# Multi-query attention: small copies ahead of the later loads, a different order of the query buffers, and GpSimd in program order

## The chip, the cores and the metric

The kernel runs on one core of a Trainium2 chip. The metric is the device time of one execution in microseconds, start to end. Before the change three runs took 775.3, 776.2 and 777.91 us, so the median is 776.2 us. The profile comes from one execution more, which took 776.08 us; its span from the first to the last instruction is 774.3 us.

Engines are named as in the profile: PE is the matrix engine (PEld its weight loads), ACT the scalar engine, DVE the vector engine, POOL GpSimd, SP the sync engine, which here only issues DMAs. A "q" behind an engine's name is its sequencer, which issues DMAs and waits on semaphores.

## The reference

There are 8 batches with 16 heads of 64 elements and 1024 positions. Keys and values have one head, shared by all query heads.

```python
# q: (8, 1024, 16, 64) float32; k, v: (8, 1024, 64) float32
q = q.transpose(0, 2, 1, 3)                       # (8, 16, 1024, 64)
scores = np.matmul(q, k[:, None].transpose(0, 1, 3, 2)) / np.sqrt(64)
weights = np.exp(scores - np.max(scores, axis=-1, keepdims=True))
weights = weights / np.sum(weights, axis=-1, keepdims=True)
out = np.matmul(weights, v[:, None]).transpose(0, 2, 1, 3)
```

## The kernel before

**Tiling.** Heads are taken two at a time, which makes 8 pairs in a batch and 64 pairs (p = 0 to 63) in all. For each pair the keys are cut into 8 tiles of 128. One score tile holds 128 keys on the partitions against 512 query positions of both heads; so a pair has 16 score tiles (8 key tiles, 2 query halves). `score` (L391) makes one with two matmuls, one per head, from `k2t` (the transposed keys, twice one above the other, one copy for each head of the pair) and `qt` (the transposed queries). The exponential of a score tile is made either on ACT (`exp_act`, L404) or on DVE by bit operations and two products (`exp_dve`, L409). The weights are then multiplied with the values in `value` (L438), where a column of ones gives the sums, and `reciprocal` and `normalise` (L458, L463) divide and store a pair's output with one DMA from SP.

**What sets the order.** `plan` (L51) is a planner in plain Python, with costs for each operation; it returns a list of operations, and the loop at L516 issues them one by one. Under `tc.manual_schedule` the instructions of PE, ACT and DVE stay in exactly this program order. POOL and SP are not in that set before the change: a scheduler orders their instructions by itself, as early as it sees fit, and can put one ahead of another that the program names first.

**Staging of queries.** Queries go through two pools of two buffers each: `qn` (natural layout, fp16) and `qt` (transposed). `load_q` (L337) issues a DMA from POOL's queue that also casts to fp16. `trans_q` (L347) issues a transposing DMA from SP's queue. Pairs 0 and 1 are each loaded alone; from pair 2 on one load and one transpose carry two pairs (`quad`, L328), so load 2 is that of pairs 2 and 3. `begin` (L491), called before the first score of a pair w, issues for even w the load of w + 4 and the transpose of w + 2. It also issues a batch ahead: the two DMAs of the next keys on POOL at the third pair of a batch (`load_k`, L299), the values on SP at the fifth (`load_v`, L308), the transpose of the keys on SP and the scaling of the values on DVE at the sixth (`trans_k`, L321, `scale_v`, L313).

**The start.** `load_first` (L356) brings batch 0's keys (`kn`) and pair 0's queries (`qf`) as fp32, plainly, without a DMA that casts or transposes. `kn` comes on SP's queue, the two halves of `qf` on ACT's and SP's. POOL casts the keys into one half of `k16` (L367). `turn_first` (L372) casts them into the other half on DVE, casts `qf` to `qn[0]` half by half on DVE, transposes on PE, and copies out of PSUM on ACT (keys) and DVE (queries). Then the first score can run.

**Who gets which buffer.** A tile gets one of its pool's buffers when its first access comes in the order of the schedule, not where its name is made. Before the change the loads of pairs 1 and 2 (L511, L512) and the transpose of pair 1 (L513) come ahead of `turn_first` (L515) in the program. Load 1 and load 2 so take the two `qn` buffers, and `qn[0]`, first written by the cast at L386, comes into the buffer of load 1 when the transpose of pair 1 has read it. In the built program, the cast of the first half of `qf` waits for three things: its own load, load 1, and the transpose of pair 1.

**Other buffers.** The output tiles (`osb`) have three buffers, and `kn` and `qf` take two of these at the start. `vn`, the raw values, has one.

Of the kernel before, what the change touches and what calls it, by code (L numbers as in the profile page):

```python
# [9 lines left out]
FP32 = mybir.dt.float32  # L10
# [4 lines left out]
ENG = mybir.EngineType  # L15

P = 128
# [229 lines left out]
def kernel(  # L247
# [7 lines left out]
    nc = tc.nc  # L255
    B, S, H, D = q.shape
    assert D == 64 and S == 1024 and H % 4 == 0
    NKT = S // P
# [9 lines left out]
    kvp = ctx.enter_context(tc.tile_pool(name="kvp", bufs=2))  # L268
    qp = ctx.enter_context(tc.tile_pool(name="qp", bufs=2))
# [37 lines left out]

    def load_v(b):  # L308
        st = kst[b]
        st["vn"] = kvp.tile([P, NKT, D], FP32, tag="vn", bufs=1, name=f"vn{b}")  # L310
        nc.sync.dma_start(out=st["vn"], in_=v[b].rearrange("(p c) d -> p c d", p=P))

    def scale_v(b):  # L313
# [14 lines left out]
    def quad(p):  # L328

        return (p,) if p < 2 else (p & ~1, p | 1)  # L330

    def queries(pool, tag, p, more):

        t = pool.tile([P, 2 * NKT + more, P], FP16, tag=tag, name=f"{tag}{p}")
        return t[:, 0 : NKT * len(quad(p)), :]

    def load_q(p):  # L337
        ps = quad(p)
        b, hp = divmod(ps[0], HP)
        qn[ps[0]] = queries(qp, "qn", p, 0)  # L340
        nc.gpsimd.dma_start(  # L341
            out=qn[ps[0]].rearrange("p (c r) x -> p c (r x)", r=len(ps)),
            in_=q[b, :, 2 * hp : 2 * hp + 2 * len(ps), :].rearrange(
                "(c p) h d -> p c (h d)", p=P),
        )

    def trans_q(p):  # L347
        ps = quad(p)
        t = queries(qtp, "qt", p, 1)
        nc.sync.dma_start_transpose(  # L350
            out=t, in_=qn[ps[0]].rearrange("p c x -> p (c x)")
        )
        for r, x in enumerate(ps):
            qt[x] = t.rearrange("p (c r) x -> p c r x", r=len(ps))[:, :, r, :]

    def load_first():  # L356
        st = kst.setdefault(0, {})
        kn = osbp.tile([P, NKT, D], FP32, tag="osb", name="kn")
        nc.sync.dma_start(out=kn, in_=k[0].rearrange("(p c) d -> p c d", p=P))
        st["qf"] = osbp.tile([P, NKT, 2 * D], FP32, tag="osb", name="qf")  # L360
        for c in range(NQC):
            (nc.scalar, nc.sync)[c].dma_start(
                out=st["qf"][:, 4 * c : 4 * c + 4, :],
                in_=q[0, QC * c : QC * c + QC, 0:2, :].rearrange("(c p) h d -> p c (h d)", p=P),
            )
        st["k16"] = kvp.tile([P, NKT, 2, D], FP16, tag="k16", name="k160")
        nc.gpsimd.tensor_copy(out=st["k16"][:, :, 1, :], in_=kn)  # L367
        st["kn"] = kn
        qn[0] = queries(qp, "qn", 0, 0)
        qt[0] = queries(qtp, "qt", 0, 1)  # L370

    def turn_first():  # L372

        st = kst[0]
        k16 = st["k16"]
        kps = psp.tile([P, NKT, P], FP16, tag="acc0", name="kps")
        qps = psp.tile([P, NKT, P], FP16, tag="acc1", name="qps")
        st["k2t"] = kvp.tile([P, NKT + 1, P], FP16, tag="k2t", name="k2t0")[:, 0:NKT, :]
        nc.vector.tensor_copy(out=k16[:, :, 0, :], in_=st["kn"])  # L379
        for c in range(NQC):  # L380
            x = slice(4 * c, 4 * c + 4)
            for i in range(4 * c, 4 * c + 4):
                nc.tensor.transpose(  # L383
                    kps[:, i, :], k16[:, i, :, :].rearrange("p r d -> p (r d)"), ident)
            nc.scalar.copy(out=st["k2t"][:, x, :], in_=kps[:, x, :])  # L385
            nc.vector.tensor_copy(out=qn[0][:, x, :], in_=st["qf"][:, x, :])  # L386
            for i in range(4 * c, 4 * c + 4):
                nc.tensor.transpose(qps[:, i, :], qn[0][:, i, :], ident)  # L388
            nc.vector.tensor_copy(out=qt[0][:, x, :], in_=qps[:, x, :])

    def score(t, c, s):  # L391
        p, j = divmod(t, NKT)
        sc[t, c] = psp.tile([P, 2, QC], FP32, tag=f"sc{s}", name=f"sc{t}_{c}")
        for h in range(2):
            nc.tensor.matmul(  # L395
                sc[t, c][:, h, :],
                kst[p // HP]["k2t"][64 * h : 64 * h + 64, j, :],
                qt[p][64 * h : 64 * h + 64, 4 * c : 4 * c + 4, :],
                start=True, stop=True, tile_position=(64 * h, 0),
            )  # L400
        if t not in wt:
            wt[t] = wtp.tile([P, 2, S], FP16, tag="wt", name=f"wt{t}")

    def exp_act(t, c):  # L404
        nc.scalar.activation(
            out=wt[t][:, :, c * QC : (c + 1) * QC], in_=sc.pop((t, c)), func=EXP, scale=ascale
        )

    def exp_dve(t, c):  # L409

        name = f"{t}"
        if c == 0:
            zs[t] = dvp.tile([P, 2, S], U16, tag="z", bufs=ZBUFS, name=f"z{name}")
        z = zs[t]
        nc.vector.tensor_scalar(
            out=z[:, :, c * QC : (c + 1) * QC], in0=sc.pop((t, c)), scalar1=vscale,
            scalar2=(15 + math.log2(C0)) * ONE, op0=ALU.mult, op1=ALU.add,
        )  # L420
        if c == 0:
            return
        V = nc.vector
        u = dvp.tile([P, 2, S], U16, tag="u", name=f"u{name}")
        m = ms[t] = dvp.tile([P, 2, S], FP16, tag="m", bufs=ZBUFS, name=f"m{name}")
        h = u.bitcast(FP16)
        steps[t] = (
            lambda: V.tensor_scalar(
                out=wt[t].bitcast(U16), in0=z, scalar1=0xFC00, scalar2=None,
                op0=ALU.bitwise_and),  # L430
            lambda: V.tensor_scalar(
                out=u, in0=z, scalar1=1023, scalar2=14 << 10,
                op0=ALU.bitwise_and, op1=ALU.bitwise_or),
            lambda: V.tensor_tensor(out=m, in0=h, in1=h, op=ALU.mult),
            lambda: V.tensor_tensor(out=m, in0=z.bitcast(FP16), in1=m, op=ALU.mult),
        )

    def value(p, grp, j, k, n, end, s):  # L438


        if n == 0:
            acc[p, grp] = psp.tile([P, QC], FP32, tag=f"acc{s}", name=f"acc{p}_{grp}")
        t = NKT * p + j
        w = (wt[t], zs[t].bitcast(FP16), ms[t])[k] if t in zs else wt[t]
        for x in range(BLOCKS[grp], BLOCKS[grp + 1]):
            i, h = divmod(x, 2)
            o = (x - BLOCKS[grp]) * (D + 1)
            nc.tensor.matmul(  # L448
                acc[p, grp][:, o : o + D + 1], w[:, h, i * P : (i + 1) * P],
                kst[p // HP]["v"][k][:, j, 0 : D + 1],  # L450
                start=(n == 0 and o == 0), stop=end, skip_group_check=True,
            )
# [5 lines left out]
    def reciprocal(p, grp):  # L458
        a = blocks(p, grp)
        rec[p, grp] = recp.tile([P, 8], FP32, tag="rec", name=f"rec{p}_{grp}")  # L460
        nc.vector.reciprocal(out=rec[p, grp][:, 0 : a.shape[1]], in_=a[:, :, D])  # L461
# [29 lines left out]
    def begin(w):  # L491
        if w % 2 == 0:
            if w + 4 < NP:
                load_q(w + 4)
            if w + 2 < NP:
                trans_q(w + 2)
        if w == 1:
            scale_v(0)
        b, hp = divmod(w, HP)
        if b + 1 < B:  # L500
            if hp == 2:
                load_k(b + 1)
            if hp == 4:
                load_v(b + 1)
            if hp == HP - 3:
                trans_k(b + 1)
                scale_v(b + 1)

    load_first()
    load_v(0)  # L510
    load_q(1)  # L511
    load_q(2)  # L512
    trans_q(1)  # L513
    with tc.manual_schedule(engines={ENG.PE, ENG.Activation, ENG.DVE}):
        turn_first()  # L515
        for _, _, (op, *args) in plan(NP, NKT)[0]:  # L516
            if op == "qk":
                while begun <= args[0] // NKT:
                    begin(begun)
                    begun += 1  # L520
                score(*args)
            elif op == "act":
                exp_act(*args)
            elif op == "z":
                exp_dve(*args)
            elif op == "step":
                steps[args[0]][args[1]]()
            elif op == "av":
                value(*args)
            elif op == "rec":  # L530
                reciprocal(*args[:2])
            else:
                normalise(*args[:2])
# [27 lines left out]
```

The softmax here doesn't subtract the row's maximum and nothing guards it: scores larger than these inputs give would overflow.

## Time and profile before

| what | measured |
|---|---|
| time, median of three runs | 776.2 us (775.3 to 777.91) |
| span of the profiled execution | 774.3 us |
| busy: ACT, PE, DVE, POOL | 750.3, 738.5, 720.4, 45.1 us |
| first exponential on ACT starts | 18.31 us |
| mean granted clock of PE | 0.991 |
| bytes moved by DMA | 75.06 MB, mean 97 GB/s |

How to read it: a busy share is a mean over the whole span, while each stage has its own limit. A row of the timeline gives the start, the duration, the engine, the line and the operation, then output and inputs by the program's names; in square brackets it gives the idle time of the engine before it and what ended that wait. The chain of work that ended last follows the releases backwards from the last instruction. The granted clock of PE is given as a share of the full one. Matmul ends are modelled, so a busy PE need not be one at its peak.

DMA landings, from issue to landing, in the first 60 us: `kn` 3.4 us, the halves of `qf` 4.2 and 4.6 us, `vn` 4.9 us, load 1 6.5 us, load 2 7.0 us, the transpose of pair 1 7.1 us.

### The profile page before, as it was taken

How to read it: one execution, taken by the hardware profiler on the slowest of the kernel's cores; microseconds unless marked ns; L12 is line 12 of the kernel's file. 1: busy time of each engine (PE TensorE's matmuls, PEld its weight loads, DVE VectorE, ACT ScalarE, POOL GpSimd, SP SyncE). 2: the span in 40 equal slices, each digit the busy share in tenths (PEclk: the TensorE clock that was granted, in tenths of full speed). 3: DMA queues.
4: the chain of work that ended last, by engine and by line, in shares of the span. 5: the costliest groups of instructions: out<-in, count | busy, mean ns of one | idle time of the engine just before them, and what ended most of it. 6: DMA issues, size and time to landing. Idle time of an engine off the chain costs nothing.

```text
span 774.3 us, 29944 instructions
## 1 busy us (share of the span) xinstructions
PE 738.5 (95%) x13616; PEld 486.3 (63%) x13616; DVE 720.4 (93%) x1043; ACT 750.3 (97%) x817; POOL 45.1 (6%) x59
## 2 busy tenths in 40 slices
PE   1899999999999999999999999999999999999997
PEld 1266666666666666666666666666666666666676
DVE  1999999999999999999999999999999999999982
ACT  1999999999999999999999999999999999999996
POOL 3100001000100001000010000000000000000000
PEclk9699999999999999999999999999999999999999
DMA  9944456556465557645585354646454546441312
GB/s 137 121 83 90 94 95 97 112 97 111 101 94 90 111 91 124 102 80 100 109 111 111 83 98 84 124 83 111 97 89 94 103 90 111 86 82 57 84 57 84
DMA packets 189839, 75.06 MB, mean 97 GB/s; under 512 B 90256, under 2 KB 188560, under 8 KB 189712
## 3 DMA queue, kind: packets, MB, share of 16 engines
q1 hardware_dynamic: 141072, 54.40, 31.4%
q0 software_dynamic: 47840, 18.35, 21.7%
q8 instruction: 106, 1.74, 1.0%
q10 hardware_dynamic: 800, 0.39, 0.2%
q14 instruction: 21, 0.17, 0.1%
HBM read 39.58 MB, written 33.55 MB: 94 GB/s over the span
## 4 chain that ended last, share of the span: by engine, by line
ACT 50%; PE 27%; DVE 16%; issue 6%; DMA 2%; POOL 0%; DVEq 0%; POOLq 0%; ACTq 0%
DMA qt_114<-qn_110 1%; DMA qn_110<-in_q_dram 1%; PE acc_0_262 L448 0%; PE acc_2_1390 L448 0%; PE acc_0_15309 L448 0%; PE acc_0_7689 L448 0%; PE acc_0_14463 L448 0%; PE acc_0_16447 L448 0%; PE acc_0_12219 L448 0%; PE acc_0_2902 L448 0%; PE acc_0_9676 L448 0%; PE acc_0_884 L448 0%; PE acc_2_16627 L448 0%; PE acc_0_17281 L448 0%; PE acc_2_17178 L448 0%
## 5 line engine op out<-in xcount | busy, mean ns | idle before, releaser
L395 PEld LDWEIGHTS <-k2t_120 64*128 64x128 f16 x256 | 13.0, 96 | 23.0 <-issue 18.4
L395 PEld LDWEIGHTS <-k2t_14746 64*128 64x128 f16 x256 | 12.8, 93 | 11.9 <-issue 6.2
L395 PEld LDWEIGHTS <-k2t_12480 64*128 64x128 f16 x256 | 12.6, 93 | 11.1 <-issue 5.3
L395 PEld LDWEIGHTS <-k2t_5706 64*128 64x128 f16 x256 | 12.6, 93 | 11.0 <-issue 5.2
L395 PEld LDWEIGHTS <-k2t_1194 64*128 64x128 f16 x256 | 12.4, 93 | 11.0 <-issue 5.4
L395 PEld LDWEIGHTS <-k2t_10207 64*128 64x128 f16 x256 | 12.4, 93 | 10.9 <-issue 5.3
L395 PEld LDWEIGHTS <-k2t_3433 64*128 64x128 f16 x256 | 12.4, 93 | 10.8 <-issue 5.2
L395 PEld LDWEIGHTS <-k2t_7972 64*128 64x128 f16 x256 | 12.2, 93 | 10.3 <-issue 4.9
L385 ACT COPY k2t_120<-kps 128x512 f16<-128x512 f16 x2 | 1.2, 586 | 13.6 <-PE kps L383 13.6
L388 PE MATMUL qps<-ident,qn_106 128*128 128x128 f16 x8 | 1.2, 308 | 10.4 <-DVE qn_106 L386 10.4
L386 DVE CAST qn_106<-qf 128x512 f16<-128x512 f32 x2 | 0.8, 421 | 10.6 <-DMA qt_114<-qn_110 10.6
L388 PEld LDWEIGHTS <-qn_106 128*128 128x128 f16 x8 | 0.7, 131 | 10.9 <-DVE qn_106 L386 10.9
L383 PE MATMUL kps<-ident,k_104 128*128 128x128 f16 x8 | 1.2, 311 | 5.1 <-POOL k_104 L367 5.1
L379 DVE CAST k_104<-kn 128x512 f16<-128x512 f32 x1 | 0.4, 427 | 4.1 <-DMA kn<-in_k_dram 4.1
L383 PEld LDWEIGHTS <-k_104 128*128 128x128 f16 x8 | 0.8, 142 | 5.1 <-POOL k_104 L367 5.1
L461 DVE RECIPROCAL rec_2_17786<-acc_2_17697 128x6 f32<-128x6 f32 x1 | 0.2, 196 | 2.6 <-PE acc_2_17697 L448 2.6
L341 POOL DMA_DIRECT2D qn_7122<-in_q_dram x1 | 1.3, 1292 | 22.7 <-DMA qt_6554<-qn_5975 22.7
L341 POOL DMA_DIRECT2D qn_1487<-in_q_dram x1 | 1.2, 1236 | 23.0 <-DMA qt_956<-qn_410 23.0
L341 POOL DMA_DIRECT2D qn_10514<-in_q_dram x1 | 1.2, 1237 | 22.9 <-DMA qt_9939<-qn_9357 22.9
L341 POOL DMA_DIRECT2D qn_8818<-in_q_dram x1 | 1.2, 1207 | 23.0 <-DMA qt_8250<-qn_7664 23.0
L461 DVE RECIPROCAL rec_0_17874<-acc_0_17769 128x6 f32<-128x6 f32 x1 | 0.2, 195 | 2.5 <-PE acc_0_17769 L448 2.5
L341 POOL DMA_DIRECT2D qn_5429<-in_q_dram x1 | 1.3, 1320 | 20.8 <-DMA qt_4858<-qn_4279 20.8
(5811 smaller groups left out, 3449.5 us busy)
## 6 DMA issues: line engine op xcount, KB each, us to landing
qn_112<-in_q_dram POOLq DMA_DIRECT2D x1, 512.0 KB, 7.0
qn_144<-in_q_dram POOLq DMA_DIRECT2D x1, 512.0 KB, 7.4
qn_410<-in_q_dram POOLq DMA_DIRECT2D x1, 512.0 KB, 6.4
qn_954<-in_q_dram POOLq DMA_DIRECT2D x1, 512.0 KB, 5.6
out_dram<-osb_450 SPq DMA_DIRECT2D x1, 512.0 KB, 4.4
out_dram<-osb_746 SPq DMA_DIRECT2D x1, 512.0 KB, 4.4
qn_1487<-in_q_dram POOLq DMA_DIRECT2D x1, 512.0 KB, 7.5
out_dram<-osb_1075 SPq DMA_DIRECT2D x1, 512.0 KB, 3.2
```

Source lines behind the costliest of these rows:

```text
L341: nc.gpsimd.dma_start(out=qn[ps[0]].rearrange("p (c r) x -> p c (r x)", r=len(ps)), in_=q[b, :, 2 * hp : 2 * hp + 2 * len(ps), :].rearrang ...
L379: nc.vector.tensor_copy(out=k16[:, :, 0, :], in_=st["kn"])
L383: nc.tensor.transpose(kps[:, i, :], k16[:, i, :, :].rearrange("p r d -> p (r d)"), ident)
L385: nc.scalar.copy(out=st["k2t"][:, x, :], in_=kps[:, x, :])
L386: nc.vector.tensor_copy(out=qn[0][:, x, :], in_=st["qf"][:, x, :])
L388: nc.tensor.transpose(qps[:, i, :], qn[0][:, i, :], ident)
L395: nc.tensor.matmul(sc[t, c][:, h, :], kst[p // HP]["k2t"][64 * h : 64 * h + 64, j, :], qt[p][64 * h : 64 * h + 64, 4 * c : 4 * c + 4, :], ...
L461: nc.vector.reciprocal(out=rec[p, grp][:, 0 : a.shape[1]], in_=a[:, :, D])
```

## The change

It has four parts.

- `load_first` now makes the tiles of pair 1's queries (`qn[1]`) and of the values (`vn`) itself, and two copies of 128x1 elements on POOL write one column of each: the first from `kn`, the second from `qf`. The loads that later fill these tiles write the same place, and so have to wait for the copies, which in turn wait for `kn` and for the first half of `qf`. `load_q` and `load_v` make their tiles only if there is none yet.
- Both halves of `qf` are now issued from ACT's queue.
- Load 2 and the transpose of pair 1 come behind `turn_first` in the program. By the first access, pair 1's tile now takes one `qn` buffer and pair 0's the other, and load 2 gets pair 0's when the casts are transposed. In the built program the cast of the first half of `qf` waits for the load of that half only. SP's order is then `kn`, values, transpose of pair 1, and so on.
- POOL joins the engines that keep program order. In the built order POOL's loads of the keys of batches 1 to 7 now each stand behind the query loads that the program names first. Before, the keys of batch 1 stood directly behind load 2, those of batches 2 and 3 around load 4, and each later one well over a batch ahead of its use; now they are issued within the batch ahead. SP is still ordered by the scheduler, and the transposes of the keys stand there nearly as before: for batch 2 between the stores of pairs 5 and 6, for batch 1 now between the transposes of loads 2 and 4 instead of ahead of both.

The orders of PE, ACT and DVE do not change, but for the second issue of `qf` on ACT.

```diff
     def load_v(b):
         st = kst[b]
-        st["vn"] = kvp.tile([P, NKT, D], FP32, tag="vn", bufs=1, name=f"vn{b}")
+        if "vn" not in st:
+            st["vn"] = kvp.tile([P, NKT, D], FP32, tag="vn", bufs=1, name=f"vn{b}")
         nc.sync.dma_start(out=st["vn"], in_=v[b].rearrange("(p c) d -> p c d", p=P))
...
     def load_q(p):
         ps = quad(p)
         b, hp = divmod(ps[0], HP)
-        qn[ps[0]] = queries(qp, "qn", p, 0)
+        if p not in qn:
+            qn[p] = queries(qp, "qn", p, 0)
         nc.gpsimd.dma_start(
...
         for c in range(NQC):
-            (nc.scalar, nc.sync)[c].dma_start(
+            nc.scalar.dma_start(
                 out=st["qf"][:, 4 * c : 4 * c + 4, :],
...
         st["kn"] = kn
         qn[0] = queries(qp, "qn", 0, 0)
+        qn[1] = queries(qp, "qn", 1, 0)
+        st["vn"] = kvp.tile([P, NKT, D], FP32, tag="vn", bufs=1, name="vn0")
+        for x, y in ((qn[1][:, 0, 0:1], kn), (st["vn"][:, 0, 0:1], st["qf"])):
+            nc.gpsimd.tensor_copy(out=x, in_=y[:, 0, 0:1])
         qt[0] = queries(qtp, "qt", 0, 1)
...
     load_first()
     load_v(0)
     load_q(1)
-    load_q(2)
-    trans_q(1)
-    with tc.manual_schedule(engines={ENG.PE, ENG.Activation, ENG.DVE}):
+    with tc.manual_schedule(engines={ENG.PE, ENG.Activation, ENG.DVE, ENG.Pool}):
         turn_first()
+        load_q(2)
+        trans_q(1)
         for _, _, (op, *args) in plan(NP, NKT)[0]:
```

## The prediction

> **What bounds the kernel now.** I read the busy times first, to find the engine that sets the steady pace.
>
> ```profile
> PE 738.5 (95%) x13616; PEld 486.3 (63%) x13616; DVE 720.4 (93%) x1043; ACT 750.3 (97%) x817; POOL 45.1 (6%) x59
> ```
>
> ACT is the fullest, and a table by stage (columns: stretch, length, busy PE, PEld, DVE, ACT, POOL, clock, DMA share, GB/s) says where its 24 us of idle time lie:
>
> ```profile
> 8.00:10.00 2.00, 0.00 (x0) 0.00 (x0) 0.00 (x0) 0.00 (x0) 0.00 (x0) 1.00 1.33 165
> 10.00:12.00 2.00, 0.00 (x0) 0.00 (x0) 0.00 (x0) 0.00 (x0) 0.00 (x0) 1.00 1.96 147
> ...
> 32.00:38.00 6.00, 6.00 (x67) 3.00 (x64) 5.18 (x6) 4.59 (x6) 0.87 (x1) 0.53 0.84 127
> ...
> 200.00:400.00 200.00, 197.27 (x3684) 130.94 (x3682) 195.06 (x283) 200.00 (x219) 14.95 (x15) 1.00 0.59 104
> ```
>
> Between 200 and 400 us ACT has no gap at all, so nothing on the DMA queues can be bought there. At the start no engine works for microseconds on end. The chain that ended last, read over the first 30 us, names the reason:
>
> ```profile
> 1.43 6.50 DMA qn_110<-in_q_dram
> 7.93 0.02 issue
> 7.95 7.10 DMA qt_114<-qn_110
> 15.05 0.03 issue
> 15.08 0.05 DVEq L386
> 15.13 0.05 issue
> 15.18 0.44 DVE qn_106 L386
> ```
>
> The load of pair 1's queries and then its DMA transpose stand ahead of the cast of pair 0's queries. The timeline shows what stood ready long before, and when pair 1's queries are first used:
>
> ```profile
> 4.14 0.43 DVE L379 CAST k_104<-kn 128x512 f16<-128x512 f32 x1 [4.14 <-DMA kn<-in_k_dram]
> 4.17 0.86 POOL L367 CAST k_104<-kn 128x512 f16<-128x512 f32 x1 [1.34 <-DMA kn<-in_k_dram]
> 5.09 0.61 PE L383 MATMUL kps<-ident,k_104 128*128 128x128 f16 x4 [5.09 <-POOL k_104 L367]
> 5.74 0.58 ACT L385 COPY k2t_120<-kps 128x512 f16<-128x512 f16 x1 [3.23 <-PE kps L383]
> 15.18 0.43 DVE L386 CAST qn_106<-qf 128x512 f16<-128x512 f32 x1 [10.61 <-DMA qt_114<-qn_110]
> ...
> 18.31 1.02 ACT L405 ACTIVATE wt_151<-sc_0_148 128x1024 f16<-128x1024 f32 x1 [0.99 <-PE sc_0_148 L395]
> ...
> 28.18 0.61 PE L395 MATMUL sc_0_233<-qt_114,k2t_120 64*128 64x512 f16 x2
> ...
> 29.20 1.13 ACT L405 ACTIVATE wt_236<-sc_0_233 128x1024 f16<-128x1024 f32 x1
> ```
>
> The DMA list gives qf's landings: its first half 0.74 + 4.2 = 4.94 us, the second 1.20 + 4.6 = 5.80. So the cast at 15.18 waited ten microseconds for a buffer, not for its data: loads 1 and 2 take the two query buffers first, and pair 0's tile gets pair 1's after that has been transposed.
>
> **What the Trainium skill says.** "TensorE: Matmul & The Clock Gate", section "Architectural detail: the array is 16× 32×32, not 1× 128×128", calls ACT and DVE strict FIFO queues: one blocked cast holds everything behind it. The trace agrees (DVE idle 10.61 us, ACT idle 10.4 us before its second copy). "DMA: Bandwidth & Descriptors", section "Issuing engines are not separate DMA queues": all issuers share the same 16 engines, so only a later issue takes a transfer out of another's way. The trace fits: qt_114's transpose took 7.1 us beside 512 KB of qn_112 and 256 KB of k_414, k2t_1194's of the same shape 3.0 us with little beside it. "TensorE: Matmul & The Clock Gate", Part 1 (the HAM clock gate), says that the matmul clock is half after an idle window of about 3.4 us and full after a busy one, the windows running freely. The trace has the clock at 0.50 from 24 to 37 us, full 4.6 us after the dense value matmuls start at 32.62.
>
> **The change part by part**, against the profiled span of 774.3 us (its run took 776.08; the others 775.3 to 777.91, median 776.2).
>
> 1. *Pair 1 gets a buffer first, load 2 comes after turn_first.* In the built order of instructions the cast of qf's first half now waits for that half's load alone, and load 2 waits for the casts and transposes of pair 0. Removed: the 10.61 us before the cast. The new start, from the rows above: kn lands at 4.14; POOL's cast ends at 5.03; PE starts on k at 5.09. The query transposes follow the first four k transposes on PE. In the trace two such batches started 0.40 apart (15.66, 16.06), so they begin at about 5.5, and their cast (4.57 or 4.94 plus 0.43) is done by 5.4. From the start of the query transposes to the first score was 15.66 to 17.66 = 2.0 us, and to the first exp 2.65. The new wait in that stretch is the second k batch behind ACT's first copy, until 5.74 + 0.58 = 6.32; that batch then ends near 7.0, about when the second query batch can start (5.5 + 1.46 = 6.96). So first exp = 5.5 + 2.65 = 8.15 in place of 18.31: gain 10.2 us.
>
> 2. *Both halves of qf on ACT's queue.* ACT issues twice, 0.46 us each, and then loads its table (1.28): done at about 3.0, needed at 5.7; hidden. kn now shares the engines with qf alone. In windows of half a microsecond the DMA moved 74, 115, 256, 316, 342 and 354 GB/s from 1.5 on, about 600 KB by 4.14, 256 of them kn's; with 768 KB in all up to then, kn lands between 0.6 us earlier and no earlier. I take 0[...] and keep -0.6 for the range. The second half is needed at about 6.5 and landed at 5.80 beside more traffic: hidden, loss bounded at 0.4.
>
> 3. *The two 128x1 copies on POOL.* No such row exists; nearest is the 128x16 memset at 0.11 us, so 0.2 for two, bounds 0.1 to 0.6. They stand behind the k cast (5.03) and qf's first half (4.94), so POOL is free for load 1 at 5.25. Queued behind them are only loads, and on SP the V load. V then lands at 5.3 + 4.9 = 10.2 at the latest (its old time), needed by scale_v at 28.77 - 10.2 = 18.6: hidden.
>
> 4. *Pair 1's load and transpose, now later.* Issued at 5.25; its load took 6.5 with the whole start beside it, 512 KB took 5.6 when alone: landing 10.8 to 11.8. Its transpose takes 3.0 (alone) to 7.1 (crowded, as before); load 2 runs beside it from about 7.6 to 15. So 13.8 to 18.9, middle 16. Needed: 28.18 - 10.2 = 18.0 for the score, and the exp behind it at 19.0 leaves a little play. Cost 0; at the worst end 18.9 + 0.65 + 0.04 - 19.0 = 0.6.
>
> 5. *Load 2, load 4 and the rest of POOL's queue.* Load 2 lands at about 7.6 + 7 = 14.6; its transpose waits for pair 0's last score (28.28 - 10.2 = 18.1) and was first used at 40.91: 8 us to spare. Load 4 waits for pair 1's transpose (16 to 19), lands by 26, and is needed at 66.6 - 10.2 = 56. Cost 0.
>
> 6. *GpSimd in program order.* The k loads of later batches are no longer run ahead: batch 2's are issued after load 14 (old clock: 115.71 + 0.9 = 116.6 to 118.4, landing within 7.5, so 126), where before they had landed long before their transpose at 113.33. That transpose stands on SP ahead of a store, so SP is held until 126 + 1.2 = 127.3:
>
> ```profile
> 113.33 1.24 SPq L324 DMA_TRANSPOSE k2t_3433<-k_2587  x1
> ...
> 128.42 0.37 SPq L483 DMA_DIRECT2D out_dram<-osb_2229  x1
> 134.49 1.86 SPq L350 DMA_TRANSPOSE qt_2585<-qn_2044  x1
> ```
>
> The next store is only ready at 128.42: hidden. In batch 1 the k transpose holds SP until about 34, the query transpose behind it could go at 31, is needed at 56: hidden. Bytes and the orders of PE, DVE and ACT are unchanged.
>
> 7. *Clock.* The stretch 32 to 38 costs ACT 6.00 - 4.59 = 1.41 us, 0.31 per microsecond of the 4.6 cold ones. One to two windows of 3.4 (the skill's figure) make 1.0 to 2.1 in the new kernel, and a clock already full at that point saves 1.4. I take 0, range -1.4 to +0.7.
>
> Sum: -10.2 + 0 + 0 = -10.2. Predicted 776.2 - 10.2 = 766.0, the span near 764.1. The likeliest case's own range is 764.2 to 767.8.
>
> **Rivals.** *Part of the gain lost near the start* (0.11): the transposes of pairs 1 or 2 land late, or the clock stays cold longer. For: 2 us of slack in step 4 is thin. Against: no longer do four loads share the engines. Were pair 1's transpose to land at 23, the gain would fall to about 6: 770; 767.8 to 773 in all. *The wait is replaced by one of equal length* (0.03): it would take a cast still held by another tile; 776. Against: the built order gives it one wait, its own load. *Slower* (0.04): SP held at a later batch's k transpose. The buffer behind the store of 128.42 is written again at 153.36, and a store takes 3.2 to 4.4, so SP must be free by 149. That decides if the k loads land after 147.6, not at 126; each microsecond more is then paid in seven batches. At 151 it makes 7 x 3.4 = 24 us: 790. Against: 21 us of slack, and the longest load in the trace took 9.0 us. *More than 12 us gained* (0.02): kn earlier and the clock full at once; 763.5.
>
> **How the numbers follow.** The likeliest case has 0.80. About 0.3%, or 2.3 us, is what a measurement of this kernel can tell from no change. Faster holds the likeliest, the partial loss and the larger gain: 0.93; same 0.03; slower 0.04. The range takes in the clock, kn's landing, the scatter of the runs and the nearer half of the partial loss: 763.7 to 768.8.
>
> **What would show it.** First exp at 8 to 8.5 us, no DMA of pair 1 in the chain at the start; DVE idle before the first query cast under 1 us; PE not waiting for qt of pair 1 at about 18; ACT without gaps from 200 to 400 us; SP's k transpose of batch 2 issued about 13 us later against the scores, without an ACT gap after it. The prediction is wrong if the first exp comes after 10, if a wait for a query transpose appears near 18 or 31, or if ACT shows idle time once per batch.

## The result and the profile after

The changed kernel takes 765.93 us (median of four runs, 764.84 to 766.71); the kernel before takes 776.33 (median of four, 775.3 to 777.91). The medians differ by 10.4 us, and the ratio is 0.9863 with a 95% interval of 0.9842 to 0.9884, so the change is about 1.4% faster. The prediction said 766.0. One of the four runs of the experiment with qf on two queues took 1024.64 us at a granted clock of 0.57; it was slow and is left out of that kernel's figures below.

The busy times of the profile after, which answer to the first line shown of before:

```profile
PE 738.3 (97%) x13616; PEld 485.9 (64%) x13616; DVE 721.2 (95%) x1043; ACT 750.0 (98%) x817; POOL 45.8 (6%) x61
```

No engine does less work: ACT's busy time is 750.0 us against 750.3, and the span is 763.1 against 774.3. What went was idle time. The chain that ended last, over the first microseconds (start, duration, what), shows where:

```profile
0.74 3.15 DMA kn<-in_k_dram
3.89 0.05 issue
3.94 0.88 POOL k_104 L369
4.82 0.05 issue
4.86 0.62 PE kps L389 x4
5.49 0.02 issue
5.51 0.59 ACT k2t_118 L391
6.10 0.04 issue
6.15 0.59 PE kps L389 x4
6.73 0.02 issue
6.75 0.61 PE qps L394 x4
```

The load and the transpose of pair 1, 13.6 us of the old chain, are gone from it. The start now runs from the key load through the key transposes and the second query batch. The timeline has the cast that used to wait, pair 1's transpose, the first exponential and the first use of pair 1:

```profile
4.78 0.44 DVE L392 CAST qn_106<-qf 128x512 f16<-128x512 f32 x1 [0.45 <-DMA qf<-in_q_dram]
...
7.94 1.02 ACT L411 ACTIVATE wt_153<-sc_0_150 128x1024 f16<-128x1024 f32 x1 [0.59 <-PE sc_0_150 L401]
...
9.83 1.32 SPq L352 DMA_TRANSPOSE qt_144<-qn_107  x1
...
17.99 0.61 PE L401 MATMUL sc_0_235<-qt_144,k2t_118 64*128 64x512 f16 x2
```

DVE waits 0.45 us instead of 10.61, and for its own data. PE does not wait for pair 1 at 17.99: no bracket stands behind the row. The stages after that (stretch, length, busy PE, PEld, DVE, ACT, POOL, clock, DMA share, GB/s):

```profile
22.00:28.00 6.00, 5.81 (x80) 2.96 (x76) 6.00 (x7) 5.50 (x6) 3.16 (x3) 1.00 0.84 134
...
190.00:390.00 200.00, 197.37 (x3678) 130.69 (x3674) 195.35 (x282) 200.00 (x220) 14.23 (x15) 1.00 0.59 102
```

The steady part is as full as before. The stretch in which the value matmuls begin costs ACT 0.50 us where it cost 1.41.

So the 11.2 us between the two profiled spans are made up of 18.31 - 7.94 = 10.37 us of an earlier first exponential, and 0.75 us less idle time on ACT in the 42 us that follow it (1.45 before, 0.70 after); 0.1 us is left over.

### The profile page after: what moved, and what is told of

Its sections match the earlier page's. It is cut to its first block, busy times and chain, and to the rows that moved or that the text cites. A ratio compares the mean times of both kernels' runs of the same rounds, so it can differ in the third digit from the quotient of the medians.

```text
span 763.1 us, 29940 instructions
## 1 busy us (share of the span) xinstructions
PE 738.3 (97%) x13616; PEld 485.9 (64%) x13616; DVE 721.2 (95%) x1043; ACT 750.0 (98%) x817; POOL 45.8 (6%) x61
## 4 chain that ended last, share of the span: by engine, by line
ACT 48%; PE 30%; DVE 16%; issue 5%; DMA 0%; POOL 0%; DVEq 0%; ACTq 0%
DMA kn<-in_k_dram 0%; PE acc_2_1392 L454 0%; PE acc_0_15311 L454 0%; PE acc_0_7691 L454 0%; PE acc_0_14465 L454 0%; PE acc_0_8537 L454 0%; PE acc_0_16449 L454 0%; PE acc_0_9678 L454 0%; PE acc_0_5447 L454 0%; PE acc_0_12221 L454 0%; PE acc_0_2904 L454 0%; PE acc_0_886 L454 0%; PE acc_0_17283 L454 0%; PE acc_2_16629 L454 0%; PE acc_2_17180 L454 0%
## 5 line engine op out<-in xcount | busy, mean ns | idle before, releaser
L304 POOL DMA_DIRECT2D k_416<-in_k_dram x2 | 2.3, 1150 | 0.0
```

The costliest lines, as they stand in the source:

```text
L304: nc.gpsimd.dma_start(out=st["k16"][:, :, r, :], in_=k[b].rearrange("(p c) d -> p c d", p=P))
```

## Experiments

The theory: pair 0's cast waited for a buffer, and the time moves one for one with the first exponential. The rivals: the crowd of early transfers delayed the start, and the copies cured it; or GpSimd's program order carries part of the gain, or costs some; or SP, held at the key transposes, has a limit which the changed kernel comes near. Each of the ten kernels ran beside the kernel before, in four groups; the ratios are to those runs, whose medians were 776.63 to 777.8. Times from different groups can be compared to about 1.5 us only.

| kernel | first exp, us | time, us | ratio to before (95%) |
|---|---|---|---|
| before | 18.31 | 776.33 | 1 |
| changed | 7.94 | 765.93 | 0.9863 (0.9842 to 0.9884) |
| changed, no copies | 8.04 | 765.79 | 0.9857 (0.9833 to 0.9881) |
| before, copies alone | 19.18 | 777.41 | 1.0009 (0.9999 to 1.0018) |
| before, third buffer | 8.00 | 768.18 | 0.9888 (0.9861 to 0.9914) |
| before, order alone | 8.57 | 766.84 | 0.9874 (0.9854 to 0.9894) |
| changed, GpSimd free | 8.12 | 766.08 | 0.9853 (0.9836 to 0.9869) |
| changed, qf on two queues | 8.10 | 765.82 | 0.9856 (0.9839 to 0.9872) |
| changed, keys 3 times | 8.14 | 766.93 | 0.9868 (0.9853 to 0.9883) |
| changed, keys 5 times | 8.41 | 766.18 | 0.9856 (0.9836 to 0.9876) |
| changed, keys 9 times | 7.92 | 818.38 | 1.0525 (1.0495 to 1.0556) |
| changed, shorter start | 7.74 | 765.32 | 0.9854 (0.9840 to 0.9868) |

**The changed kernel without the copies**

```diff
-        qn[1] = queries(qp, "qn", 1, 0)
-        st["vn"] = kvp.tile([P, NKT, D], FP32, tag="vn", bufs=1, name="vn0")
-        for x, y in ((qn[1][:, 0, 0:1], kn), (st["vn"][:, 0, 0:1], st["qf"])):
-            nc.gpsimd.tensor_copy(out=x, in_=y[:, 0, 0:1])
```

> The changed kernel without the two small copies: load 1 and the V load start at once, beside the keys and pair 0's queries; buffer order, ACT's two issues and GpSimd's program order stay. If the buffer order is the cause: keys land near 4.1 us instead of 3.9, first exponential at 8.2 us (7.94 in the changed kernel), time 766.2 us, at most 0.5 above the changed kernel. If the traffic at the start is the cause: the two halves of the queries land late, first exponential after 10 us, time above 768 us.

Measured: 765.79 us, first exponential at 8.04. The cast of the keys starts at 3.99 us, 0.08 later than with the copies, and that is all that holding back load 1 and the values bought. The copies are not the cause.

**The kernel before with the copies alone**

```diff
         qn[0] = queries(qp, "qn", 0, 0)
+        qn[1] = queries(qp, "qn", 1, 0)
+        st["vn"] = kvp.tile([P, NKT, D], FP32, tag="vn", bufs=1, name="vn0")
+        for x, y in ((qn[1][:, 0, 0:1], kn), (st["vn"][:, 0, 0:1], st["qf"])):
+            nc.gpsimd.tensor_copy(out=x, in_=y[:, 0, 0:1])
```

> The kernel before with the two small copies alone: load 2 and the transpose of pair 1 stay ahead of pair 0's casts, so pair 0 still gets pair 1's buffer. If the buffer order is the cause: the cast still waits for pair 1's transpose, whose load is now issued only at about 6 us; it lands near 12.5, the transpose near 19, first exponential near 22 us against 18.3: slower than before by 3 to 5 us, 780 us. If the copies are the cause: faster than before, 766 to 770 us.

Measured: 777.41 us, 20 runs of it against 23 of before: a loss of about 0.1%, at most 0.2%, with zero just inside the interval. I had expected 3 to 5 us. The cast waits for pair 1's transpose, as expected; the size was wrong. From its timeline:

```profile
12.80 1.32 SPq L352 DMA_TRANSPOSE qt<-qn  x1
...
16.06 0.43 DVE L392 CAST qn<-qf 128x512 f16<-128x512 f32 x1 [11.67 <-DMA qt<-qn]
```

The load came late, as reckoned, but the transpose, issued at 12.80, had been read out by 16.06. It took 3.1 us and not 7. By then loads 1 and 2 had landed and only the tail of batch 1's keys was still coming in, which is the likely reason. Holding the loads back lengthened the first part of the wait and shortened the second: first exponential 0.87 us later, median 0.77 us above the 776.64 measured beside it.

**The kernel before with a third query buffer**

```diff
-    qp = ctx.enter_context(tc.tile_pool(name="qp", bufs=2))
+    qp = ctx.enter_context(tc.tile_pool(name="qp", bufs=3))
```

> The kernel before with three query buffers instead of two and nothing else: no tile has to wait for another one's buffer at the start, while loads 1 and 2 and the keys of batch 1 still run beside the first loads. If the buffer is the cause: the cast of pair 0's queries waits for its own load alone, first exponential near 8.3 us, time 766 us, within 1 us of the changed kernel. If the crowded start is the cause: first exponential after 10 us and at most half of the 10 us gained.

Measured: first exponential at 8.00 us, time 768.18. From its timeline:

```profile
4.82 0.43 DVE L386 CAST qn<-qf 128x512 f16<-128x512 f32 x1 [0.42 <-DMA qf<-in_q_dram]
...
8.59 1.33 SPq L350 DMA_TRANSPOSE qt<-qn  x1
```

The cast waits for its own load, and pair 1's transpose is issued only after it. One more buffer, with no line moved, takes the wait away, while loads 1 and 2 still start as early as before (load 2 at 4.82 us); with the order alone, below, that settles the cause. The median is 1.3 to 2.4 us above the other kernels without the wait (766.84 and 765.79 beside it, 765.93 changed), while its runs spread from 766.04 to 769.46 and its profiled span is only 764.2. Where the rest goes was not settled: the scheduler also ordered GpSimd's later loads anew (the keys of batch 1 from 14.35 us instead of 5.88), so this is not the buffer alone.

**The kernel before with the order alone**

```diff
-    load_q(2)
-    trans_q(1)
     with tc.manual_schedule(engines={ENG.PE, ENG.Activation, ENG.DVE}):
         turn_first()
+        load_q(2)
+        trans_q(1)
```

> The kernel before with load 2 and the transpose of pair 1 moved behind pair 0's turn and nothing else: no copies, the query halves on two queues, GpSimd ordered by the scheduler. If the buffer order is the cause: first exponential at 8.2 to 8.5 us, 766 us, all of the gain. If GpSimd's program order or the copies carry part of it: 768 us or more.

Measured: 766.84 us, first exponential at 8.57. Moving two calls brings 9.8 us over the kernel before beside it, where the whole change brought 10.4. The first exponential is 0.63 us later than in the changed kernel, mostly because the key cast starts at 4.46 us and not 3.91: this is the part that keeping other loads off the start can account for, at most 0.6 us, and kernels with the same crowd (no copies, third buffer) had the keys at 3.97 to 3.99.

**The changed kernel with GpSimd left to the scheduler**

```diff
-    with tc.manual_schedule(engines={ENG.PE, ENG.Activation, ENG.DVE, ENG.Pool}):
+    with tc.manual_schedule(engines={ENG.PE, ENG.Activation, ENG.DVE}):
```

> The changed kernel with GpSimd ordered by the scheduler again: the first key load of batch 1 now goes ahead of load 1, and the later keys are loaded early again. If the order of GpSimd's loads is hidden: first exponential at 7.9 to 8.1 us, time within 0.5 us of the changed kernel, 766 us; the transpose of batch 2's keys is issued earlier against the scores and nothing else moves. Rival, that the program order of GpSimd costs or saves time in each batch: a difference of 1 us or more, spread over the seven batches.

Measured: 766.08 us. In time it cannot be told from the changed kernel, but the profile is not the same, and the expectation that nothing else moves was wrong. Its timeline:

```profile
5.38 1.02 POOL L304 DMA_DIRECT2D k<-in_k_dram  x1
6.39 0.96 POOL L343 DMA_DIRECT2D qn<-in_q_dram  x1
7.34 1.74 POOL L304 DMA_DIRECT2D k<-in_k_dram  x2
9.08 0.90 POOL L343 DMA_DIRECT2D qn<-in_q_dram  x1
...
20.12 1.46 PE L401 MATMUL sc<-qt,k2t 64*128 64x512 f16 x6 [2.06 <-DMA qt<-qn]
...
20.77 6.69 ACT L411 ACTIVATE wt<-sc 128x1024 f16<-128x1024 f32 x7 [1.55 <-PE sc L401]
```

Left free, GpSimd puts one key load ahead of load 1 and two behind it. Pair 1's transpose is then issued at 11.95 instead of 9.83 and takes some 8 us to land; PE waits 2.06 us for it and ACT 1.55. This is the prediction's rival of a partial loss, at the very place it named, but in a kernel without the fourth part of the change. Program order on GpSimd thus does a small service at the start, 1.55 us of ACT's time in the profiled run, which the medians of four runs do not resolve.

**The changed kernel with qf on two queues**

```diff
-            nc.scalar.dma_start(
+            (nc.scalar, nc.sync)[c].dma_start(
```

> The changed kernel with the second half of pair 0's queries on SP's queue again. If it is hidden, as the sum said: first exponential within 0.2 us of 7.94, time within 0.4 us of the changed kernel. Rival, that one queue keeps the second half out of the keys' way: keys land 0.2 us later, and the first exponential moves by as much.

Measured: 765.82 us (median of three runs), keys cast at 4.00, first exponential at 8.10, 0.16 later. Where the second half of qf is issued does not matter to what a time can show.

**The keys of each batch loaded three, five and nine times**

```diff
-        for r in range(2):
+        for r in [0, 1] * 3:      # or * 5, or * 9
             nc.gpsimd.dma_start(
                 out=st["k16"][:, :, r, :], in_=k[b].rearrange("(p c) d -> p c d", p=P)
```

The loads repeat the same data into the same place, each behind the one before. (The comment in the cut is not in the kernels.)

> The changed kernel with the two key loads of each batch issued three times over, each waiting for the one before it, so that the keys land some 14 us later (batch 2: near 129 us instead of 114). The transpose of the keys holds SP until then, with one store and the next query transpose behind it. The slack reckoned for the slower rival is 21 us, from the store's buffer: so the time stays within 1 us of the changed kernel, 766 us. If SP's wait were already at its limit: 7 times some 10 us, above 800 us.

> As the one with three issues, with five: the keys land some 30 us later (batch 2: near 144 us). That is beyond the slack of some 21 us by 8 to 10 us in each of seven batches: 55 to 75 us slower than the changed kernel, 820 to 840 us, with ACT gaps once per batch and DVE waiting for the output buffer. If the slack is larger than reckoned: 766 to 775 us.

> The changed kernel with the two key loads of each batch issued nine times over. With five, the transpose of batch 2's keys went out at 131.7 us, 7.0 us later than with three, so 3.5 us for each further pair: with nine near 146 us. The store behind it has to leave by about 139 us in this kernel's clock (its buffer is written again at 143.5). If the slack of the slower rival was reckoned rightly: some 6 to 8 us lost in each of six or seven batches, 800 to 825 us, DVE waiting for the output buffer and ACT with gaps once per batch. If the slack is larger: 766 to 770 us.

Measured: with three, 766.93 us, and batch 2's key transpose at 124.69 in place of 114.28 us; hidden, though the median is 1.0 above the changed kernel's. With five, 766.18, transpose at 131.72. I had expected 30 us of delay and a heavy loss; a repeat costs less than a first load (3.5 us for each pair), so the delay was 17.4 us, inside the slack. With nine, 818.38. The waits of that kernel (who, for whom, us in total, times, longest), then its timeline at batch 2 and at batch 4:

```profile
ACT wt L411 <- PE sc L401: 52.8, 21, 8.4
DVE osb L476 <- DMA out_dram<-osb: 27.2, 4, 8.4
PE sc L401 <- DMA qt<-qn: 17.0, 3, 8.5
```

```profile
149.81 1.23 SPq L325 DMA_TRANSPOSE k2t<-k  x1
151.21 2.01 SPq L352 DMA_TRANSPOSE qt<-qn  x1
...
155.62 1.04 PE L401 MATMUL sc<-qt,k2t 64*128 64x512 f16 x4 [8.47 <-DMA qt<-qn]
...
156.33 1.94 ACT L411 ACTIVATE wt<-sc 128x1024 f16<-128x1024 f32 x2 [8.31 <-PE sc L401]
```

```profile
359.85 1.23 SPq L325 DMA_TRANSPOSE k2t<-k  x1
361.13 3.77 SPq L489 DMA_DIRECT2D out_dram<-osb  x2
...
367.49 0.56 DVE L476 TENSOR_TENSOR osb<-acc,rec 128x384 f32<-128x384 f32 x1 [8.37 <-DMA out_dram<-osb]
...
370.88 1.94 ACT L411 ACTIVATE wt<-sc 128x1024 f16<-128x1024 f32 x2 [8.12 <-PE sc L401]
```

ACT's waits of 52.8 us, of which the changed kernel has 1.3, are nearly the whole loss of 818.38 - 765.93 = 52.5. The large ones, 4.3 to 8.4 us, come in six places, once per batch from batch 2 on. The mechanism of the slower rival is real: in all six SP stands at the key transpose, and what is queued behind it comes late. In four of them (batches 3, 4, 6 and 7) it is a store, and DVE waits for the store's buffer: the victim that I had named. In the other two (batches 2 and 5) the query transpose stood next in SP's queue, and PE waited for that; in batch 2 the scheduler had put pair 6's store ahead of the key transpose.

By this run the key transpose of batch 2 may go out at 149.81 - 8.3 = 141.5 us before ACT pays. This kernel's exponentials were 1.2 us behind the changed kernel's by then, and there the transpose goes at 114.28: some 26 us to spare. The same reckoning gives 26 us for batch 5 and 30 to 33 us where the store was the victim. The five-fold load shows 17.4 us of it outright.

**A shorter start**

```diff
+        warm = psp.tile([P, QC], FP32, tag="sc0", name="warm")
+        for _ in range(28):
+            nc.tensor.matmul(warm[:, 0:P], ident, ident, start=True, stop=True)
         nc.vector.tensor_copy(out=k16[:, :, 0, :], in_=st["kn"])
+        nc.scalar.copy(out=k16[:, :, 1, :], in_=st["kn"])
...
-        nc.gpsimd.tensor_copy(out=st["k16"][:, :, 1, :], in_=kn)
```

and in `turn_first` all key transposes, then both query casts, ACT's copies, all query transposes, both copies of qt.

> The changed kernel with a shorter start: ACT instead of GpSimd casts the second half of the keys, all key transposes go ahead of the query transposes so that none waits for ACT's copy, both casts of pair 0's queries go ahead of the copies, and 28 matmuls on the identity whose result nothing reads keep PE busy from about 1.5 to 4.5 us so that its clock is full at the first transpose. If time is one for one with the first exponential: first exponential at 6.6 to 7.2 us against 7.94, time 764.6 to 765.3 us. If the clock falls back before the value matmuls start at about 21 us: their cold stretch costs the same 0.7 us of ACT as in the changed kernel. Rival, that the early matmuls delay the key transposes: first exponential at 8 us or later.

Measured: 765.32 us (five runs), first exponential at 7.74. It is the lowest median, but its interval overlaps the changed kernel's. Of the 0.7 to 1.3 us by which the first exponential was expected earlier, only 0.20 came. The timeline shows where the rest went:

```profile
4.70 0.43 DVE L394 CAST qn<-qf 128x512 f16<-128x512 f32 x1 [0.42 <-DMA qf<-in_q_dram]
...
5.11 1.01 POOL L343 DMA_DIRECT2D qn<-in_q_dram  x1
...
5.50 0.84 DVE L394 CAST qn<-qf 128x512 f16<-128x512 f32 x1 [0.38 <-DMA qf<-in_q_dram]
5.63 1.07 ACT L396 COPY k2t<-kps 128x512 f16<-128x512 f16 x2 [1.16 <-PE kps L390]
6.39 0.23 PEld L399 LDWEIGHTS <-qn 128*128 128x128 f16 x4 [0.65 <-DVE qn L394]
```

The second cast, now early enough to meet GpSimd's issue of load 1, took twice as long as the first, and before it waited for the second half of qf. The clock was full for the second query batch and the first scores; scores begun at 8.82 still took 0.39 us, those at 9.73 took 0.61.

**All runs together.** In every profiled run the span is the start of the first exponential, plus ACT's idle time in the following 42 us, plus a constant: 754.5 us before, 754.5 after, 754.2 to 754.9 in seven others. Without the copies and with the keys three times, about 1.5 and 1.0 us of idle time later in the run are added. Only the kernel with nine key loads is outside, for its gaps once per batch. This is what "one for one" means here.

The idle time in those 42 us is not a property of the kernel alone. It goes, roughly, with the moment at which the clock becomes full, which the trace's clock events give: 2.2 us after the first value matmul in the changed kernel (0.70 us idle), 2.8 with the keys five times (0.90), 4.1 with the shorter start and with the third buffer (1.39 and 1.62), 4.4 with the order alone (2.10), 5.0 before (1.45). With GpSimd free it is 4.9 us and 2.44 idle, which holds the wait for pair 1 too. Of all twelve profiled runs the changed kernel's had the earliest full clock.

## Why the prediction was right

1. *The buffer wait.* Right, and shown by the third buffer and by the order alone. First exponential predicted at 8.15, measured at 7.94: the keys were there at 3.89 us instead of 4.14. The query transposes began at 5.28 (5.5 reckoned); from there to the exponential it took 2.66 us (2.65 reckoned). The chain passes through the second key batch and ACT's first copy, the new wait that the step had named. That the median met 766.0 to within 0.1 us is in part luck: four runs of this kernel scatter over 1.9 us.

2. *Two issues of qf on ACT.* Hidden, as said; its table load began at 1.79 and the first copy at 5.51. The keys' gain was within the 0 to 0.6 us given.

3. *The copies.* 0.18 and 0.38 us, within the bounds; load 1 was issued at 5.25 us, the number predicted. The values landed at 5.29 + 2.8 = 8.1.

4. *Pair 1.* Load 4.6 us and transpose 5.3, so it landed at 15.1 (middle estimate 16, needed at 17.99). The load was quicker than the 5.6 which I had taken as its least, from twice the bytes. The slack was 2.9 us, and the free GpSimd used it up and 2 us more: calling it thin was right. The range of 3.0 to 7.1 us for the transpose did not hold in that kernel, where it took some 8.

5. *Load 2 and later.* Issued at 7.67 (7.6) and landed at 14.2 (14.6); no wait.

6. *GpSimd's order and SP.* SP was held at batch 2's key transpose until 114.28 + 1.23 = 115.5, the next store was issued at 117.11: hidden, by less than 2 us up to the store and by some 26 us up to any cost. Against the first exponential the key transpose went out 11.3 us later than before (about 13 forecast). The limit was reckoned from the store's buffer (21 us); the nine-fold load showed it there in four batches, at 30 us or more, and at the query transpose in two, at 26. The reckoning took stores to last 3.2 to 4.4 us; the trace before has two of 8.2 and 7.2, so its 149 us was less sure than it looked. The run with nine was expected to lose 6 to 8 us in each of six or seven batches; it lost 4.3 to 8.4 in six.

7. *The clock.* Taken at 0 within -1.4 to +0.7; in the profiled run -0.75. This is mainly why that span fell 11.2 us and not 10.2. The medians fell 10.4. The estimate rested on what the Trainium skill states ("TensorE: Matmul & The Clock Gate", Part 1); here full speed returned less than 3 us after the value matmuls began at 22.43, read from the matmuls' own durations (0.61 to 0.39 us). The table of stages reads 1.00 even before that, because the trace's first clock event is the change to full at 24.61. In the kernel before the clock became full at 37.64, which is 5.0 us after 32.62 and not the 4.6 that the step used. The twelve profiled runs lie between 2.2 and 5.0 us, about half of them below the one window of 3.4 that the step took as its least for a cold start; that the changed kernel's run drew 2.2 was luck.

## What to carry to other kernels

When an engine waits long for a DMA whose data it does not use, ask which tile held its buffer: buffers go out in the order of first access, and a prefetch named ahead of the first work can take the buffer that this work needs. One buffer more is the quick test, a later prefetch the cure. And to price a queue that is put in program order, find what stands behind its waiting instruction on each queue, and delay the cause step by step until it costs.

## What the runs showed of the hardware

- DVE and GpSimd's issue of a DMA can hold each other up; which one waits goes by how far the issue is when the DVE step begins. In the changed kernel a DVE step on 128x2048, 0.68 us alone, kept 0.69 when it began 0.16 us after a key issue, and the issue took 1.32 us in place of 0.87. Steps begun 0.32 and 0.33 us after an issue took 1.05 and 1.03, and the issue its 0.87. The cast of 128x512 from fp32 to fp16 that took 0.84 us in the shorter start began 0.39 us after an issue; begun within 0.06 us of one (third buffer, order alone, GpSimd free) it took its usual 0.42 to 0.43. The Trainium skill, "DMA: Bandwidth & Descriptors", section "SWDGE vs HWDGE vs iDMA", says that GpSimd writes its descriptors into memory from which DVE, in one of its modes, locks it out; the lengthened issues fit this, and the lengthened DVE steps show that DVE is made to wait as well.
- The same transpose of 128x1024 took 3.0 us with little beside it, 5.3 beside one load, and 7 to 8 beside several, while one of twice the size (that of load 2, before) took 4.3: the neighbours set its time more than its size.
- 28 matmuls in a row over 3.2 us did not make the clock full at once: the eight key transposes behind them took 1.06 us, and the second query batch was the first to be fast (0.40 against 0.61). By the trace's clock events it was full from 5.94 to 9.35 us and then fell back, although PE had no gap over 0.7 us. In the kernel before it was full from 20.58 to 23.99 and fell back with no gap over 0.6 us. So no idle window of 3.4 us, which the prediction had taken from the Trainium skill, stood before these falls.
